# A token store on another queue, token sums in smaller pieces, a square on DVE, and first loads of the second product inside the last pair

## The chip, the cores and the metric

The kernel runs on one core of a Trainium2 chip, in fp32. The metric is the device time of one execution in microseconds, as the median over several runs. The core has five engines with ordered queues: PE (matrix products), DVE (vector operations), ACT (activations, and here also the rounding copies), POOL (further vector operations) and SP, which in this kernel only issues DMA transfers. An instruction waits at the head of its engine's queue, and all that is behind it waits too.

## What is computed

One layer of a diffusion backbone on 1152 tokens (128 of context, 1024 latent), width 1024. The change touches its last third. `mix` is the sum of two gated branches; then, with a layer norm `LN`:

```
x  = LN(ALPHA*x + gate1 * (mix @ w_out)) * ln_g[0] + ln_b[0]      # kept as x2
u  = LN(x) * (1 + scale2) + shift2
hid = square(relu(u @ w_fc + b_fc))                                # 1152 x 4096
x  = LN(ALPHA*x + gate2 * (hid @ w_proj + b_proj)) * ln_g[1] + ln_b[1]
```

## The kernel before

Products in fp32 precision are made of three passes of a rounded type: every operand is split into `hi`, a rounded copy made by ACT (line 67 in `split`, line 1053 for u), and `lo`, the rest, made by a subtraction on DVE or POOL (lines 68, 1055). `mm3` (lines 111 to 113) then issues hi x hi, hi x lo and lo x hi. The order of all instructions is written out by hand; within an engine they run in the order in which the program issues them.

*Output projection* (`branches`, from line 1011). For each of nine token tiles t, `wout(t)` issues 48 matmuls, then `cols(t-3)`, `chain(t)` and `chain2(t-1)`. `chain` loads the old x (`xr`, SP, line 988), multiplies by the gate and adds (DVE, 994 and 995), takes the statistics, normalises (ACT) and applies ln_g and ln_b (POOL, 999 and 1000; DVE for the last tile). `chain2` stores x2 (SP, 1005), takes new statistics and normalises into `z`. `cols` turns z by eight transposes on PE (1044), scales and shifts into `u` (ACT 1051, from tile 6 on half of it on DVE 1049), makes hi (ACT 1053), stores u to DRAM in `u_d` (SP, 1054) and returns the lo part (DVE 1055), which `wout` issues after `chain`. z has three buffers, u one. The tiles 6 to 8 are turned later, between the first groups of the first feed-forward product, which are issued at the end of `branches` (1069 to 1079).

*First feed-forward product* (`ffn1`). The 32 column blocks of w_fc go in 16 pairs. The first two pairs are plain products: six groups remain here, each ended by a relu and a square on ACT (1149, 1150); a pair is stored to `h_d` on SP (1095). Pairs 2 to 15 use seven products instead of eight on 2x2 blocks (a Strassen scheme in the Winograd form), which need sums of token blocks (`Th`, `Tl`) and of weight blocks. The token sums are the generator `sums(s)`, s the half of the tokens: four loads of quarters of u_d (1111), four differences of 128x1152 elements (1118) and their hi and lo parts (1122 on ACT, 1124 on POOL or DVE). Four steps of the generator are issued behind each of the six groups, the rest behind the store of pair 1. Then come the first weights of pair 2 (`load`, 1167; `prep`). For a pair, `steps` lists 14 products, each with what follows it: copies of a bank (`keep`, ACT 1239), adds (DVE 1248), relus (ACT 1092), and `end`, the square of one half of the tokens (ACT 1253, 128x1152). Each is followed by `store`.

*Second feed-forward product* (`ffn2`). It runs in eight blocks b of four k tiles. `ahead(b)` loads four rows of h into the buffer of the lo parts (1291), then, four times, a weight (1300, two staging buffers `ws`) and its split, and the split of one row of h. `ahead(0)` is issued whole ahead of the first product, behind the bias `bp` (1281).

```
for _ in ahead(0):
    pass
```

Of the kernel before, what the change touches and what calls it, by code (L numbers as in the profile page):

```python
# [9 lines left out]
F = mybir.dt.float32  # L10
R = mybir.dt.float32r
# [28 lines left out]
class Kern:  # L40
# [871 lines left out]
    def branches(self, st, hrp):  # L912
# [90 lines left out]
        def chain2(t):  # L1003
            y = ys.pop(t)
            nc.sync.dma_start(self.x2_d[t], y)
            mv = self.ln_stats(y)
            z = p3.tile([128, D], F, name="z", tag="z", bufs=3)
            self.normalise(z, y, mv)
            xn[t] = z

# [20 lines left out]
        def cols(t, bank=self.pj):  # L1031
            c, o = t // 3, (t % 3) * 128
            if t % 3 == 0:
                h, l = self.hilo(c)
                self.hi.append(h)
                self.lo.append(l)
            z = xn.pop(t)
            u = p3.tile([128, KT, 128], F, name="u", tag="u", bufs=1)
            j = 1 if t else 0
            for g in range(2):  # L1040
                tp = bank()
                for i in range(4):
                    k = 4 * g + i
                    nc.tensor.transpose(tp[:, i * 128:(i + 1) * 128], z[:, k * 128:(k + 1) * 128], self.ident)
                for i in range(4):
                    k = 4 * g + i
                    q = tp[:, i * 128:(i + 1) * 128]
                    if t >= 6 and g == 1:
                        nc.vector.tensor_scalar(u[:, k, :], q, m2[:, 1, k, j:j + 1], m2[:, 0, k, j:j + 1], OP.mult, OP.add)
                    else:  # L1050
                        nc.scalar.activation(u[:, k, :], q, AF.Identity, scale=m2[:, 1, k, j:j + 1], bias=m2[:, 0, k, j:j + 1])  # L1051
            h, l = self.hi[c][:, :, o:o + 128], self.lo[c][:, :, o:o + 128]
            nc.scalar.activation(h, u, AF.Copy)
            nc.sync.dma_start(self.u_d[:, :, t * 128:(t + 1) * 128], u)
            return lambda: nc.vector.tensor_tensor(l, u, h.bitcast(F), OP.subtract)  # L1055

        self.hi, self.lo = [], []
# [24 lines left out]
    def ffn1(self, st):  # L1082
# [18 lines left out]
        self.r0s.close()  # L1101
        pt = self.pool(st, "tt")
        Th, Tl = [pt.tile([128, 4, 4, 2 * HN], R, name=n) for n in ("Th", "Tl")]
        tmp = ExitStack()
        ptmp = self.pool(tmp, "tmp")
        B = lambda a, k, s, j: a[:, 4 * k:4 * k + 4, 2 * HN * s + HN * j:2 * HN * s + HN * j + HN]

        def sums(s):
            f = lambda a, i: a.bitcast(F)[:, i, :, HN * s:HN * s + HN]
            for o, k, j in ((f(Tl, 0), 0, 1), (f(Th, 0), 0, 0), (f(Tl, 1), 1, 1), (f(Th, 3), 1, 0)):  # L1110
                nc.sync.dma_start(o, B(self.u_d, k, s, j))
            yield
            g, v = nc.gpsimd, nc.vector
            d = {}

            def diff(i, x, y, e):
                d[i] = ptmp.tile([128, 4, HN], F, name="T", tag="T", bufs=3)
                e.tensor_tensor(d[i], x, y, OP.subtract)

            def part(i, e):  # L1120
                h, l = Th[:, i, :, HN * s:HN * s + HN], Tl[:, i, :, HN * s:HN * s + HN]
                nc.scalar.activation(h, d[i], AF.Copy)
                yield
                e.tensor_tensor(l, d[i], h.bitcast(F), OP.subtract)
                yield

            diff(2, f(Tl, 1), f(Tl, 0), g)
            yield
            diff(0, f(Tl, 0), f(Th, 0), v)
            yield  # L1130
            diff(1, f(Tl, 1), d[0], v)
            yield
            yield from part(2, g)
            yield from part(0, v)
            diff(3, f(Th, 3), d[1], v)
            yield
            yield from part(1, g)
            yield from part(3, v)

        work = (x for s in range(2) for x in sums(s))  # L1140
        for p in range(2):
            for i in range(2):
                w = self.fcw[2 * p + i] if 2 * p + i < 3 else self.w_next(("fc", 3), 0)
                for c in range(NC):
                    if c < 2 and 2 * p + i < 3:
                        continue
                    ps = self.group(w, c)
                    o = Hs[p][:, i, c * C:(c + 1) * C]
                    relu(o, ps, 2 * p + i)
                    nc.scalar.activation(o, o, AF.Square)  # L1150
                    for _ in range(4):
                        next(work, None)
            store(p, Hs[p])
        for _ in work:
            pass
        tmp.close()
        pe = self.pool(st, "ev")


        raw, ready, pos = {}, [], [None, 0]  # L1160
# [49 lines left out]
        def need(n):  # L1210
            while len(ready) < n and next(weights, 0) is None:
# [5 lines left out]
        P = {1: ("A11", pair(0, 0)), 5: ("S1", tt(0)), 6: ("S2", tt(1)), 7: ("S3", tt(2)),  # L1217
             2: ("A12", pair(1, 0)), 4: ("A22", tt(3)), 3: ("S4", pair(1, 1))}
        need(8)
        for p in range(2, 16):  # L1220
            H = new_h()
            base = 7 * (p - 2)
# [27 lines left out]

            def end(s):
                q = H[:, :, 2 * HN * s:2 * HN * s + 2 * HN]
                nc.scalar.activation(q, q, AF.Square)

            steps = [(1, 0, "A", True, lambda: keep(1, 0)), (1, 1, "A", True, lambda: keep(1, 1)),
                     (5, 0, "C", True, None), (6, 0, "A", False, lambda: keep(2, 0)),
# [9 lines left out]
            for i, (n, s, b, first, after) in enumerate(steps):  # L1266
                mul(n, s, b, first)
                if after:
                    after()
                if i % 2:  # L1270
                    need(base + 8 + i // 2 + 1)
            store(p, H)


    def ffn2(self, st):
        nc, I, O = self.nc, self.I, self.O
        self.lo_pool = False
        p = self.pool(st, "ffn")
        acc = [p.tile([128, D], F, name=f"acc{t}") for t in range(NT)]
        bp = p.tile([128, D], F, name="bp", tag="bp")  # L1280
        nc.sync.dma_start(bp, I["b_pr"].to_broadcast([128, D]))
        rows = {}
        gate = lambda t: rows["g2l" if t else "g2c"]
        x2s = {}
        ws = {}
        NS = 8

        def load_h(b):
            for i in range(4):
                o = 4 * (b % 2) + i  # L1290
                nc.sync.dma_start(self.X[1][:, o, :].bitcast(F), self.h_d[2 * b + i // 2][:, i % 2, :])

        def split_h(b, i):
            o = 4 * (b % 2) + i
            h, l = self.X[0][:, o, :], self.X[1][:, o, :]
            self.split(h, l, l.bitcast(F))

        def weight(b, i):
            s = self.ring.tile([128, 1024], F, name="ws", tag="ws", bufs=2)
            nc.sync.dma_start(s, I["w_pr"][4 * b + i])  # L1300
            if b % 2:
                w = p.tile([128, 2, 1024], R, name="w", tag="w2", bufs=4)
            else:
                w = self.ring.tile([128, 2, 1024], R, name="w", tag="w", bufs=4)
            self.split(w[:, 0], w[:, 1], s, nc.gpsimd if b else None)
            ws[b, i] = w

        def ahead(b):
            if b >= NS:
                return  # L1310
            load_h(b)
            yield
            for i in range(4):
                weight(b, i)
                yield
                split_h(b, i)
                yield

        def proj(b, t):
# [21 lines left out]
            if t:  # L1341
                nc.vector.scalar_tensor_tensor(acc[t - 1], x2s.pop(t - 1), ALPHA, acc[t - 1], OP.mult, OP.add)

        for _ in ahead(0):
            pass
        sa = ExitStack()
        self.sides.append(self.ada_rest(self.pool(sa, "ada"), range(6, 8)))
        for b in range(NS - 1):
# [130 lines left out]
```

## Time and profile before

| | us |
|---|---|
| median of 3 runs | 2325.74 (2325.53 to 2326.64) |
| the profiled execution | 2322.08 |
| its span, first to last instruction | 2320.0 |
| PE busy | 2161.7 (93%) |
| DVE, ACT, POOL busy | 1289.8, 947.2, 650.9 (56%, 41%, 28%) |
| mean granted clock of PE | 0.972 |

Times of the trace count from the start of the span. In the rows, `PE pj L112` is a matmul of line 112 into the tile `pj`; `SPq` is SP's queue of transfers; `[12.06 <-DVE lo L1055]` means that the engine was idle for 12.06 us before, and that an instruction of line 1055 on DVE ended it. The clock is a share of full speed (1.00 is the 2.4 GHz level, 0.50 the 1.2 GHz one). A matmul's length in the timeline is longer than its distance to the next one, since they overlap.

### The profile page before, as it was taken

The page shows a single profiled execution, that of the slowest core. Times are in us where ns is not written, and L with a number is a line of the kernel's source. Part 1 is how long each engine was busy: PE and PEld are TensorE (multiplying, and loading weights), DVE is VectorE, ACT ScalarE, POOL GpSimd, SP SyncE. Part 2 cuts the span into 40 slices and gives each one's busy share as a digit, 9 for nine tenths or more (in the row PEclk, how much of TensorE's full clock was granted, in tenths as well). Part 3 has the DMA queues.
Part 4 walks back from the last instruction along what each step waited for, and adds up shares of the span by engine and source line. Part 5 has one row for each costly group of instructions (what it writes and reads, how often), then busy time and mean ns, then how long its engine had stood idle before and what let it go on. Part 6 is the DMA issues. An engine that isn't in the chain of part 4 may idle for free.

```text
span 2320.0 us, 31633 instructions
## 1 busy us (share of the span) xinstructions
PE 2161.7 (93%) x12723; PEld 2031.2 (88%) x12723; DVE 1289.8 (56%) x2096; ACT 947.2 (41%) x1500; POOL 650.9 (28%) x349
## 2 busy tenths in 40 slices
PE   7988999999999999999899998589999969999996
PEld 4888999999999999999899987579999958888885
DVE  4364775775674546887625465552333326643378
ACT  5454424414524426777613234354555441121112
POOL 1402212311420312233302042343333302331176
PEclk9999999999999999999999999789999979999998
DMA  6121241142122130111432323352222244322342
GB/s 265 37 70 38 71 142 54 61 135 75 60 94 79 41 96 28 46 46 67 154 97 88 141 83 102 98 177 87 95 100 101 93 153 146 114 95 78 128 145 82
DMA packets 96754, 223.83 MB, mean 96 GB/s; under 512 B 20132, under 2 KB 48420, under 8 KB 93536
## 3 DMA queue, kind: packets, MB, share of 16 engines
q1 hardware_dynamic: 84368, 209.16, 26.8%
q10 hardware_dynamic: 12240, 12.66, 1.6%
q8 instruction: 99, 1.62, 0.3%
q14 instruction: 47, 0.39, 0.1%
HBM read 171.70 MB, written 50.09 MB: 96 GB/s over the span
## 4 chain that ended last, share of the span: by engine, by line
PE 74%; DVE 8%; DMA 6%; ACT 3%; issue 2%; SPq 1%; POOL 0%; ACTq 0%; DVEq 0%
PE pj L111 16%; PE pj L112 16%; PE pj L113 16%; PE pps L113 5%; PE pps L112 5%; PE pps L111 5%; DMA out_n<-nt 2%; PE xb L111 1%; PE xb L112 1%; PE xb L113 1%; DMA xr<-in_x 1%; PE wps L113 1%; PE wps L112 1%; PE wps L111 1%; ACT u L1051 1%
## 5 line engine op out<-in xcount | busy, mean ns | idle before, releaser
L111 PE MATMUL pj<-hi,w 128*128 128x384 f32 (+1 forms) x2120 | 706.4, 333 | 23.6 <-ACT w L67 9.4
L112 PE MATMUL pj<-lo,w 128*128 128x384 f32 (+1 forms) x2120 | 703.2, 332 | 20.4 <-DVE lo L1055 12.1
L113 PE MATMUL pj<-hi,w 128*128 128x384 f32 (+1 forms) x2120 | 702.4, 331 | 0.8 <-POOL w L68 0.8
L111 PEld LDWEIGHTS pj<-hi,w 128*128 128x128 f32 x2120 | 404.3, 191 | 26.1 <-ACT u L1051 10.0
L112 PEld LDWEIGHTS pj<-lo,w 128*128 128x128 f32 x2120 | 404.2, 191 | 21.2 <-DVE lo L1055 12.3
L113 PEld LDWEIGHTS pj<-hi,w 128*128 128x128 f32 x2120 | 403.9, 190 | 1.2 <-POOL w L68 1.2
L68 POOL TENSOR_TENSOR w<-ws,w 128x1024 fp32r<-128x1024 f32 (+1 forms) x91 | 184.1, 2028 | 573.8 <-ACT w L67 531.7
L67 ACT ACTIVATE w<-ws 128x1024 fp32r<-128x1024 f32 (+1 forms) x175 | 159.0, 914 | 379.8 <-DMA ws<-in_w_pr 282.5
L111 PE MATMUL pps<-w,hi 128*128 128x512 f32 x576 | 225.5, 391 | 19.9 <-ACT hi L67 19.9
L113 PE MATMUL pps<-w,lo 128*128 128x512 f32 x576 | 225.4, 391 | 1.4 <-DVE lo L68 1.4
L112 PE MATMUL pps<-w,hi 128*128 128x512 f32 x576 | 225.2, 391 | 0.0
L68 DVE TENSOR_TENSOR w<-ws,w 128x1024 fp32r<-128x1024 f32 (+1 forms) x84 | 104.8, 1254 | 113.6 <-ACT w L67 112.7
L1334 DVE TENSOR_TENSOR acc<-pps,acc 128x512 f32<-128x512 f32 x108 | 73.7, 690 | 142.9 <-PE pps L113 142.9
L111 PEld LDWEIGHTS pps<-w,hi 128*128 128x128 f32 x576 | 108.8, 189 | 42.9 <-ACT hi L67 20.5
L111 PE MATMUL pj<-Th,w 128*128 128x288 f32 x448 | 134.2, 300 | 9.3 <-ACT e L1239 9.3
L112 PE MATMUL pj<-Tl,w 128*128 128x288 f32 x448 | 132.7, 296 | 0.0
L113 PE MATMUL pj<-Th,w 128*128 128x288 f32 x448 | 132.6, 296 | 0.0
L113 PEld LDWEIGHTS pps<-w,lo 128*128 128x128 f32 x576 | 108.6, 189 | 25.5 <-DVE lo L68 3.2
L112 PEld LDWEIGHTS pps<-w,hi 128*128 128x128 f32 x576 | 108.8, 189 | 22.7
L716 POOL TENSOR_TENSOR CS<-Cst,CS 128x516 fp32r<-128x516 f32 x56 | 74.2, 1326 | 184.1 <-ACT CS L715 180.2
L1248 DVE TENSOR_TENSOR Hf<-pj,e 128x288 f32<-128x288 f32 x84 | 36.6, 454 | 143.5 <-ACT e L1239 88.7
L464 POOL PARTITION_ALL_REDUCE aacc<-aacc x16 | 56.2, 3556 | 195.4 <-DVE aacc L463 169.4
(313 smaller groups left out, 4082.5 us busy)
## 6 DMA issues: line engine op xcount, KB each, us to landing
ws<-in_w_in SPq DMA_DIRECT2D x56, 512.0 KB, 4.1
h<-Hf SPq DMA_DIRECT2D x16, 1152.0 KB, 4.8
lo<-h SPq DMA_DIRECT2D x32, 576.0 KB, 3.8
aw<-in_w_ada SPq DMA_DIRECT2D x64, 256.0 KB, 3.6
ws<-in_w_fc SPq DMA_DIRECT2D x32, 512.0 KB, 3.4
ws<-in_w_pr SPq DMA_DIRECT2D x32, 512.0 KB, 4.2
gm<-gs ACTq DMA_DIRECT2D x48, 192.0 KB, 1.9
gmr<-gm SPq DMA_DIRECT2D x16, 576.0 KB
```

The source lines that it names most:

```text
L67: self.nc.scalar.activation(hi, x, AF.Copy)
L68: (eng or self.nc.vector).tensor_tensor(lo, x, hi.bitcast(F), OP.subtract)
L111: mm(out, lhsT=ah, rhs=bh, start=first, stop=False, skip_group_check=onto)
L112: mm(out, lhsT=ah, rhs=bl, start=False, stop=False, skip_group_check=onto)
L113: mm(out, lhsT=al, rhs=bh, start=False, stop=last, skip_group_check=onto)
L464: nc.gpsimd.partition_all_reduce(acc[j], acc[j], channels=128, reduce_op=ReduceOp.add)
L716: nc.gpsimd.tensor_tensor(CS[d][1], Cst[d], CS[d][0].bitcast(F), OP.subtract)
L1051: nc.scalar.activation(u[:, k, :], q, AF.Identity, scale=m2[:, 1, k, j:j + 1], bias=m2[:, 0, k, j:j + 1])
L1248: nc.vector.tensor_tensor(o, bank[b, s][:, :HN], ev[e, s], OP.add)
L1334: nc.vector.tensor_tensor(acc[t][:, s], pss[n], (acc[t] if b else bp)[:, s], OP.add)
```

## The change

Four edits. The store of u is issued by ACT's queue, and u is written into the buffer of z, which now has four buffers (before: three of z and one of u). The token sums are made per k tile, in pieces of 128x288, with tiles of the pool `ev`, and five steps of the generator are issued behind each group. The square at the end of a half pair is a product on DVE. The helpers of the second product become methods, and in the last pair (p = 15) `early(i)` issues, behind step i, the four loads of h (i = 1), the splits of its four rows (6, 8, 10, 12) and the first two weights with their splits (7, 10); the other two weights are issued at the start of `ffn2`, behind the load of `bp`.

```diff
     def chain2(t):
-            z = p3.tile([128, D], F, name="z", tag="z", bufs=3)
+            z = p3.tile([128, D], F, name="z", tag="z", bufs=4)
     def cols(t, bank=self.pj):
             z = xn.pop(t)
-            u = p3.tile([128, KT, 128], F, name="u", tag="u", bufs=1)
+            u = z.rearrange("p (k t) -> p k t", t=128)
...
             nc.scalar.activation(h, u, AF.Copy)
-            nc.sync.dma_start(self.u_d[:, :, t * 128:(t + 1) * 128], u)
+            nc.scalar.dma_start(self.u_d[:, :, t * 128:(t + 1) * 128], u)
...
-        tmp = ExitStack()
-        ptmp = self.pool(tmp, "tmp")
+        pe = self.pool(st, "ev")
     def sums(s):
...
-            d = {}
-
-            def diff(i, x, y, e):
-                d[i] = ptmp.tile([128, 4, HN], F, name="T", tag="T", bufs=3)
-                e.tensor_tensor(d[i], x, y, OP.subtract)
-
-            def part(i, e):
-                h, l = Th[:, i, :, HN * s:HN * s + HN], Tl[:, i, :, HN * s:HN * s + HN]
-                nc.scalar.activation(h, d[i], AF.Copy)
-                yield
-                e.tensor_tensor(l, d[i], h.bitcast(F), OP.subtract)
-                yield
-
-            diff(2, f(Tl, 1), f(Tl, 0), g)
-            yield
-            diff(0, f(Tl, 0), f(Th, 0), v)
-            yield
-            diff(1, f(Tl, 1), d[0], v)
-            yield
-            yield from part(2, g)
-            yield from part(0, v)
-            diff(3, f(Th, 3), d[1], v)
-            yield
-            yield from part(1, g)
-            yield from part(3, v)
+            for k in range(4):
+                q = lambda a, i: f(a, i)[:, k, :]
+                d = {}
+
+                def diff(i, x, y, e):
+                    d[i] = pe.tile([128, HN], F, name="e", tag="e", bufs=6)
+                    e.tensor_tensor(d[i], x, y, OP.subtract)
+
+                def part(i, e):
+                    h, l = (a[:, i, k, HN * s:HN * s + HN] for a in (Th, Tl))
+                    nc.scalar.activation(h, d[i], AF.Copy)
+                    e.tensor_tensor(l, d[i], h.bitcast(F), OP.subtract)
+
+                diff(2, q(Tl, 1), q(Tl, 0), g)
+                diff(0, q(Tl, 0), q(Th, 0), v)
+                diff(1, q(Tl, 1), d[0], v)
+                yield
+                diff(3, q(Th, 3), d[1], v)
+                part(2, g)
+                part(0, v)
+                yield
+                part(1, g)
+                part(3, v)
+                yield
...
                     nc.scalar.activation(o, o, AF.Square)
-                    for _ in range(4):
+                    for _ in range(5):
                         next(work, None)
             store(p, Hs[p])
         for _ in work:
             pass
-        tmp.close()
-        pe = self.pool(st, "ev")
...
+        def early(i):
+            if i == 1:
+                self.load_h(0)
+            if i in (6, 8, 10, 12):
+                self.split_h(0, (i - 6) // 2)
+            if i in (7, 10):
+                self.weight(0, (i - 7) // 3)
...
             def end(s):
                 q = H[:, :, 2 * HN * s:2 * HN * s + 2 * HN]
-                nc.scalar.activation(q, q, AF.Square)
+                nc.vector.tensor_tensor(q, q, q, OP.mult)
...
                 if i % 2:
                     need(base + 8 + i // 2 + 1)
+                if p == 15:
+                    early(i)
             store(p, H)
...
+    def load_h(self, b):
+        for i in range(4):
+            o = 4 * (b % 2) + i
+            self.nc.sync.dma_start(self.X[1][:, o, :].bitcast(F), self.h_d[2 * b + i // 2][:, i % 2, :])
+    def split_h(self, b, i):
+        o = 4 * (b % 2) + i
+        h, l = self.X[0][:, o, :], self.X[1][:, o, :]
+        self.split(h, l, l.bitcast(F))
+    def weight(self, b, i):
+        s = self.ring.tile([128, 1024], F, name="ws", tag="ws", bufs=2)
+        self.nc.sync.dma_start(s, self.I["w_pr"][4 * b + i])
...
+        self.split(w[:, 0], w[:, 1], s, self.nc.gpsimd if b else None)
+        self.ws2[b, i] = w
     def ffn2(self, st):
...
-        for _ in ahead(0):
-            pass
+        self.weight(0, 2)
+        self.weight(0, 3)
```

## Rows read from the trace of the kernel before

**Rows 1.** Busy time by stretch: from:to, length, PE, PEld, DVE, ACT, POOL, PEclk, DMA, GB/s

```profile
1426.00:1512.00 86.00, 54.48 (x233) 47.37 (x234) 46.52 (x73) 38.17 (x69) 25.90 (x9) 0.80 0.32 98
1567.00:1885.00 318.00, 310.85 (x2316) 308.57 (x2316) 95.03 (x148) 159.65 (x311) 103.98 (x78) 1.00 0.24 90
1885.00:1915.00 30.00, 8.74 (x23) 5.56 (x23) 10.25 (x9) 10.04 (x10) 0.00 (x0) 0.60 0.75 270
```

**Rows 2.** Timeline of PE: start, length, line, matmul; in brackets the idle before

```profile
1500.72 0.69 PE L112 MATMUL pj<-lo,w 128*128 128x384 f32 x1 [12.06 <-DVE lo L1055]
...
1555.75 0.61 PE L111 MATMUL pj<-hi,w 128*128 128x288 f32 x1 [9.45 <-ACT w L67]
...
1904.91 0.80 PE L111 MATMUL pps<-w,hi 128*128 128x512 f32 x1 [19.89 <-ACT hi L67]
```

**Rows 3.** Chain of waits in the output projection: start, length, what

```profile
1390.65 0.87 PE pj L1044 x8
1402.44 0.88 PE pj L1044 x8
...
1431.70 5.12 DMA xr<-in_x
1436.91 1.24 DVE y L995
...
1445.46 2.91 ACT u L1051 x8
1448.96 5.30 DMA xr<-in_x
...
1490.08 1.24 DVE y L995
```

**Rows 4.** Waits of SP's queue, 1390 to 1520: total, times, longest

```profile
SPq L1054 <- ACT u L1051: 76.9, 7, 15.3
```

**Rows 5.** Timeline of SP's queue in the output projection

```profile
1414.24 15.63 SPq L62 DMA_DIRECT2D ws<-in_w_fc  x2
...
1448.39 0.52 SPq L1054 DMA_DIRECT2D u_d<-u  x1
...
1449.72 1.02 SPq L1005 DMA_DIRECT2D x<-y  x1
```

**Rows 6.** Timeline of POOL: a product-stage sum and one of the sums

```profile
1444.22 3.29 POOL L1000 TENSOR_TENSOR y<-y,bn 128x1024 f32<-128x1024 f32 x1
...
1536.80 3.30 POOL L1124 TENSOR_TENSOR Tl<-T,Th 128x1152 fp32r<-128x1152 f32 x1 [0.45 <-ACT Th L1122]
```

**Rows 7.** Timeline of DVE: two differences of the sums

```profile
1527.04 1.36 DVE L1118 TENSOR_TENSOR T<-Tl,Th 128x1152 f32<-128x1152 f32 x1 [6.76 <-DMA Th<-u_d]
...
1537.49 3.83 DVE L1118 TENSOR_TENSOR T<-Th,T 128x1152 f32<-128x1152 f32 x1
```

**Rows 8.** Groups by form: count, busy us, mean ns, idle before

```profile
L1248 DVE TENSOR_TENSOR Hf<-pj,e 128x288 f32<-128x288 f32 x84 | 36.6, 454 | 143.5 <-ACT e L1239 88.7 <-PE pj L113 54.8
...
L68 POOL TENSOR_TENSOR w<-ws,w 128x512 fp32r<-128x512 f32 x42 | 56.4, 1343 | 136.1 <-ACT w L67 136.1
```

**Rows 9.** Timeline of ACT at both passages

```profile
1547.45 0.56 ACT L1092 ACTIVATE Hf<-pj,pack 128x384 f32<-128x384 f32 x1
...
1555.07 0.63 ACT L67 ACTIVATE w<-ws 128x512 fp32r<-128x512 f32 x1 [1.29 <-DMA ws<-in_w_fc]
...
1902.74 1.06 ACT L67 ACTIVATE w<-ws 128x1024 fp32r<-128x1024 f32 x1 [15.47 <-DMA ws<-in_w_pr]
```

**Rows 10.** Timeline of SP's queue at both passages

```profile
1549.02 1.34 SPq L1167 DMA_DIRECT2D ws<-in_w_fc  x2
...
1866.52 21.10 SPq L1095 DMA_DIRECT2D h<-Hf  x2
1887.66 0.44 SPq L1281 DMA_DIRECT2D bp<-in_b_pr  x1
...
1892.33 1.17 SPq L1300 DMA_DIRECT2D ws<-in_w_pr  x2
```

More of the change, by code (lines that the diff above doesn't have):

```diff
@@ L1219, in ffn1 @@
         need(8)
+        self.ws2 = {}
+        def early(i):
[5 more added lines that the diff above has]
+                self.weight(0, (i - 7) // 3)
         for p in range(2, 16):
@@ L1271, in ffn1 @@
                     need(base + 8 + i // 2 + 1)
+                if p == 15:
+                    early(i)
             store(p, H)
+    def load_h(self, b):
[9 more added lines that the diff above has]
+        self.nc.sync.dma_start(s, self.I["w_pr"][4 * b + i])
+        if b % 2:
+            w = self.p2.tile([128, 2, 1024], R, name="w", tag="w2", bufs=4)
+        else:
+            w = self.ring.tile([128, 2, 1024], R, name="w", tag="w", bufs=4)
+        self.split(w[:, 0], w[:, 1], s, self.nc.gpsimd if b else None)
+        self.ws2[b, i] = w
     def ffn2(self, st):
@@ L1277, in ffn2 @@
         self.lo_pool = False
-        p = self.pool(st, "ffn")
+        p = self.p2 = self.pool(st, "ffn")
         acc = [p.tile([128, D], F, name=f"acc{t}") for t in range(NT)]
@@ L1284, in ffn2 @@
         x2s = {}
-        ws = {}
+        ws = self.ws2
         NS = 8
[L1288 to L1306, printed above, removed]
         def ahead(b):
-            if b >= NS:
-                return
-            load_h(b)
+            self.load_h(b)
             yield
             for i in range(4):
-                weight(b, i)
+                self.weight(b, i)
                 yield
-                split_h(b, i)
+                self.split_h(b, i)
                 yield
```

## Prediction

> **What bounds the kernel now.** I first read the busy line of the page: PE works for 93% of the span, so only the places where it stands still can be won. The stretch table names them: the stage of the output projection (PE busy 54.48 of 86 us, clock 0.80) and the passage between the two feed-forward products (8.74 of 30 us, clock 0.60) [rows 1]. The PE timeline then gives the large holes and what ended them: 12.06 us before the lo part of the sixth token tile, 9.45 us before the first weight of the pairs, 19.89 us before the second product [rows 2].
>
> The chain of waits says why the first stage is slow. Its period is one load of x: 1431.70 to 1448.96 is 17.26 us, of which xr takes 5.12; then y, its statistics, z, then u on ACT (1445.46 + 2.91 = 1448.37), and at 1448.96 the next xr starts [rows 3]. SP shows the link: the store of u goes out at 1448.39, and only behind it comes the load [rows 5]; that store waited on ACT's u seven times, 76.9 us in all [rows 4]. So a load which needs nothing of u is released by u. Without this, one tile costs PE 11.79 us (1390.65 to 1402.44, while PE was ahead) [rows 3].
>
> **The change part by part.**
>
> *Token store on ACT's queue, u written into z.* SP's order becomes xr(t), x2(t-1), xr(t+1). x2(t-1) needs POOL's sum, some 10.6 us behind y's start (1436.91 to 1444.22 + 3.29) [rows 3, 6]; but this loop spans two tiles, so with 1 us of issue and 5.3 us of load it asks for about 8.5 us per tile. The engines' own orders: on DVE the way from y (1436.91) to where ACT takes u up (1445.46) is 8.55 us [rows 3], with the gate multiplies (as many columns as y, so some 1.3) about 9.9; ACT has u 2.91, hi (1024 columns, as the split of 1.06 [rows 9]), the issue of the store 0.53 (SP's price [rows 5]) and under 6 for y, z and two roots, 10.3 us. Both lie under PE's 11.79. So PE sets the pace: the product of tile 3 ends at 1390.65, that of tile 8 at 1390.65 + 5 x 11.79 = 1449.6. One hitch remains: SP's two weight loads at 1414.24 hold the queue 15.63 us, because the second waits for a DVE split [rows 5]; tile 5's xr stays behind it. I put that split at about 1416 in the new order, so y of tile 5 comes near 1422.5 instead of 1415; with a DVE order of 9.9 us against 11.79 three tiles win back most of it, and y of tile 8 comes at 1452.5 against 1490.08 [rows 3]: 37.6 us earlier. What follows (the lo part that ends the 12.06 us hole) keeps its order. That hole shrinks to 2 to 4 us and gives back some 1.4 us of half clock. Store waits of u in the three late tiles (about 2 us each) hid under PE and bring nothing. Sum: -39 us; -34 if DVE and POOL collide once per tile, -43 if PE never stands still.
>
> *Sums in pieces.* Before, DVE and POOL had 16 operations of 1152 columns; now they have 64 of 288. DVE and POOL keep each other out: DVE's subtraction costs 1.36 alone and 3.83 from 1537.49; POOL's began at 1536.80 and ended at 1540.10, and 1540.10 + 1.36 is close to DVE's end at 1541.32 [rows 6, 7]. So their times add. Each k piece has five DVE operations of 0.454 and three of POOL; POOL's nearest row is 1.34 for 512 columns, 0.78 if it scales to 288 [rows 8]. 5 x 0.454 + 3 x 0.78 = 4.6, with handoffs 4.85, for eight pieces 38.8 us. They begin where DVE's first sum did, 1527.04 [rows 7], plus some 1.4 because the load into Tl should now wait for the landing of the last u (it overlays z): end near 1567.
> That alone PE would not feel, as it needs the sums only six steps into the pair. But five pieces per group instead of four are now issued, 25 of 26 of them ahead of the last group's relu on ACT's ordered queue. Before, that relu ran at 1547.45 [rows 9]; now it stands behind the hi parts of the last k piece, about 1564. Behind it come the square, the store of the pair, and on SP the first weight load of the pairs (1549.02), whose landing (1555.07) ended PE's hole [rows 9, 10]. All move by 16.5 us; collisions with the sums saved later give back 1 to 1.5. Sum: +15. Bounds: +4 if DVE and POOL overlapped fully, +27 if a small POOL operation cost the whole 1.34.
>
> *Square on DVE.* 28 squares of 1152 columns, 1.36 each [rows 7], 38 us on DVE, which is busy 95.03 of 318 in the pairs, while PE is busy 310.85 [rows 1]. PE's short stalls there wait on ACT's copies behind weight splits, not on squares. Cost 0; if DVE's cover were gone, at most the 0.2 us by which it is longer than ACT's at the last store, and a wait for POOL of up to 1.3; taken together -2 to +2.
>
> *First loads and splits in the last pair.* The cost before: the square ends, the pair's store goes out, bp at 1887.66, four loads of h, and the weight load at 1892.33; its split starts at 1902.74 [rows 9, 10]. Now the four h loads leave right behind the store of the pair before (1866.52 [rows 10]; the first two steps of the pair have read the buffer). The old train of bp, four loads and a weight behind a store took 1887.66 to 1902.74, 15.1 us; without bp I take 13.5, so the first weight lands near 1880. From there ACT's and DVE's queues are one ping-pong, because each split stands ahead of the pair's own adds and relus: w 1.06 and hi 1.2 by its columns on ACT [rows 9], lo 1.36, w 1.24 as y's [rows 3], adds 0.454, two squares 1.36 on DVE [rows 7, 8]: 11 us of DVE, 17 with the handoffs. The step that reuses the bank of the last copy is met to within 1 us. But the last store leaves at 1897 instead of just ahead of 1887.66, and the third weight stands behind it and bp on SP: half of the old train, 7.5 us, so 1904.5, split by 1905.6. PE does the first half of the first product early (2.7 us), waits, and ends its 24 matmuls near 1911 against 1915.6. Sum: -4.5. Bounds: -12 if the handoffs cost nothing and the store is not late; +2 if the first weight lands 3 us later and PE waits for the copy in the pair.
>
> **Total.** -39 + 15 + 0 - 4.5 = -28.5 on the profiled execution's 2322.08: 2293.6. The median of the runs lies 3.66 above that execution, so the prediction is 2297 for it.
>
> **Rivals.**
> *Only the issue time is saved (slower).* If xr merely found another thing ahead of it, x2 of the tile before, the period would stay: xr 5.9, y to POOL's end 10.6, issue 1, 17.5 us. Then moving nine stores saves 9 x 0.53 = 4.8 us and the rest gives -4.8 + 15 - 4.5 = +5.7: 2331. It decides as soon as the stage wins less than 10.5 us. For it: x2 is on the same queue. Against: it goes out at 1449.72, right behind xr [rows 5], and the next xr is a tile later. The Trainium skill (DMA: Bandwidth & Descriptors, Issuing engines are not separate DMA queues) says that starting transfers from several engines saves only the sequencer's time to start them, usually small; by that rule this rival would hold. The row of the 76.9 us wait speaks against it, since here the queue's order, not its issue time, is the cost.
> *The sums stay cheap.* DVE and POOL interleave at this size and T costs +4: 2286. For it: the pieces let ACT start sooner; against: the 3.83 us row.
> *The passage closes.* The splits hide wholly and PE waits only for the last two weights: -15 there, 2287. Against: the third weight is still behind the last store.
> *u in place binds PE to ACT.* If the second four transposes waited for the first four u's, as both touch one buffer, the loop would be 11.1 of products, 1.5 of u and about 1.1 of transposes, 13.7 us: five tiles lose up to 9.5, less the 2.9 that tile 5 lost anyway: 2304.
>
> **Chances.** My forecast 0.5, with its own range 2285 to 2311; cheap sums 0.18; closed passage 0.12; in-place wait 0.1; issue time only 0.06; others 0.04. Range: 2277 to 2314, which takes in the first four and leaves the tails of the POOL price and of the slower rival. 0.2% (4.7 us) is about what a measurement of this kernel tells from no change. Faster 0.90, same 0.04, slower 0.06.
>
> **What would show it.** Right: xr loads leave without u ahead, about 11.8 us apart, and the hole before the lo part is under 4 us; the last relu of the groups runs some 16 us behind PE's last group and the hole of 9.45 grows to about 25; the second product starts its first four blocks directly behind the last pair and then waits 14 us for the third weight. Wrong: xr still 17 us apart; the hole before the pairs at 9 to 14 us; the last store at its old distance from the last matmul.

## The result and the profile after

The changed kernel takes 2290.2 us (median of 4 runs, 2287.31 to 2291.59), the kernel before 2326.19 beside it (4 runs): a ratio of 0.9844, 95% interval 0.9827 to 0.9861, so 36 us faster. The prediction was 2297 with a range of 2277 to 2314. The profiled execution of the changed kernel took 2287.31 us, its span is 2285.5 against 2320.0.

The three stretches of [rows 1], of the same lengths and, to within about 1 us, at the same places of the work, which now come earlier by 37, 29 and 31 us:

```profile
1389.00:1475.00 86.00, 81.89 (x407) 71.59 (x406) 66.50 (x102) 52.83 (x98) 36.37 (x13) 0.96 0.42 135
1538.00:1856.00 318.00, 310.00 (x2322) 307.79 (x2322) 138.37 (x177) 135.35 (x287) 115.30 (x78) 1.00 0.27 100
1854.00:1884.00 30.00, 13.02 (x36) 9.04 (x35) 11.38 (x12) 8.74 (x11) 0.44 (x1) 0.60 0.56 205
```

In the output projection PE is now busy 81.89 of 86 us at a clock of 0.96, against 54.48 at 0.80. In the pairs, DVE went from 95 to 138 us busy and ACT from 160 to 135: the squares and, at the end, the splits. In the passage to the second product PE still stands for more than half of the 30 us.

The timeline of PE has the holes that answer to [rows 2]:

```profile
1463.78 0.69 PE L112 MATMUL pj<-lo,w 128*128 128x384 f32 x1 [4.11 <-DVE lo L1055]
...
1527.00 0.61 PE L111 MATMUL pj<-hi,w 128*128 128x288 f32 x1 [17.58 <-ACT w L67]
...
1856.87 0.50 PE L111 MATMUL pps<-w,hi 128*128 128x512 f32 x1 [1.74 <-ACT w L67]
...
1874.64 0.80 PE L111 MATMUL pps<-w,hi 128*128 128x512 f32 x1 [13.70 <-ACT w L67]
```

12.06 became 4.11; 9.45 became 17.58; and the one wait of 19.89 became three, 1.74, 1.08 and 13.70, of which the last stands in the middle of the first product.

SP's queue in the output projection, beside [rows 5]:

```profile
1403.12 12.83 SPq L62 DMA_DIRECT2D ws<-in_w_fc  x2
1416.01 0.42 SPq L988 DMA_DIRECT2D xr<-in_x  x1
1416.52 0.38 SPq L1005 DMA_DIRECT2D x<-y  x1
1417.00 0.38 SPq L988 DMA_DIRECT2D xr<-in_x  x1
...
1432.68 0.37 SPq L988 DMA_DIRECT2D xr<-in_x  x1
...
1443.19 0.38 SPq L988 DMA_DIRECT2D xr<-in_x  x1
```

No store of u stands between the loads of x any more. The one thing that still holds them is the pair of weight loads, 12.83 us. With it DVE waits for a load of x once, 3.61 us, and three tiles later it has caught up: y of tile 8, whose row was 1490.08 in [rows 3], comes at 1452.58.

```profile
1421.54 1.23 DVE L995 SCALAR_TENSOR_TENSOR y<-xr,y 128x1024 f32<-128x1024 f32 x1 [3.61 <-DMA xr<-in_x]
...
1452.58 1.78 DVE L995 SCALAR_TENSOR_TENSOR y<-xr,y 128x1024 f32<-128x1024 f32 x1
```

ACT's queue at the start of the pairs, beside [rows 9]: the relu of the last group now stands behind hi parts of the sums (line 1123), several of which wait for a difference.

```profile
1515.44 1.01 ACT L1123 ACTIVATE Th<-e 128x288 fp32r<-128x288 f32 x2 [0.54 <-DVE e L1119]
1517.98 0.78 ACT L1123 ACTIVATE Th<-e 128x288 fp32r<-128x288 f32 x2 [1.54 <-POOL e L1119]
1518.67 0.56 ACT L1092 ACTIVATE Hf<-pj,pack 128x384 f32<-128x384 f32 x1
1519.26 0.52 ACT L1148 ACTIVATE Hf<-Hf 128x384 f32<-128x384 f32 x1
1519.69 0.76 ACT L1123 ACTIVATE Th<-e 128x288 fp32r<-128x288 f32 x2
1526.32 0.63 ACT L67 ACTIVATE w<-ws 128x512 fp32r<-128x512 f32 x1 [5.87 <-DMA ws<-in_w_fc]
```

PE's last group had ended at 1509.43, so the relu is 9.2 us late (before: 1.15). Behind the square, on SP, go the store and the load of the first weight, beside [rows 10]; and at the end of the pairs the store of the last pair, bp, and the third and fourth weight:

```profile
1519.81 0.33 SPq L1095 DMA_DIRECT2D h<-Hf  x1
1520.25 1.34 SPq L1163 DMA_DIRECT2D ws<-in_w_fc  x2
...
1864.53 0.33 SPq L1095 DMA_DIRECT2D h<-Hf  x1
1864.94 0.38 SPq L1310 DMA_DIRECT2D bp<-in_b_pr  x1
1865.42 2.11 SPq L1296 DMA_DIRECT2D ws<-in_w_pr  x2
```

### The profile page after: what moved, and what is told of

Same layout as the page of the kernel before. It is cut to its first block, busy times and chain, and to the rows that moved or that the text cites. A ratio compares the mean times of both kernels' runs of the same rounds, so it can differ in the third digit from the quotient of the medians.

```text
span 2285.5 us, 31722 instructions
## 1 busy us (share of the span) xinstructions
PE 2150.3 (94%) x12723; PEld 2021.9 (88%) x12723; DVE 1333.9 (58%) x2154; ACT 922.3 (40%) x1496; POOL 666.7 (29%) x367
## 5 line engine op out<-in xcount | busy, mean ns | idle before, releaser
L112 PEld LDWEIGHTS pj<-lo,w 128*128 128x128 f32 x2120 | 402.7, 190 | 12.5 <-DVE lo L68 8.1
L1341 DVE TENSOR_TENSOR acc<-pps,acc 128x512 f32<-128x512 f32 x108 | 73.7, 691 | 146.6 <-PE pps L113 146.5
L111 PEld LDWEIGHTS pj<-Th,w 128*128 128x128 f32 x448 | 84.0, 188 | 11.5 <-ACT e L1246 11.5
```

The costliest lines, as they stand in the source:

```text
L111: mm(out, lhsT=ah, rhs=bh, start=first, stop=False, skip_group_check=onto)
L112: mm(out, lhsT=ah, rhs=bl, start=False, stop=False, skip_group_check=onto)
L1341: nc.vector.tensor_tensor(acc[t][:, s], pss[n], (acc[t] if b else bp)[:, s], OP.add)
```

## Experiments

Each experiment is the changed kernel with the edit shown. The runs were made on three chips. On these the kernel before took 2328 us instead of 2326, and in the experiments' traces the first load of x came at 1358 to 1365 us instead of 1354, with nothing edited ahead of it. So the ratios are compared with that of the changed kernel run again on the last chip (0.9851), and the traces by stages that begin at that load. All lengths are us, from PE's and SP's timelines: A from the first load of x to the sixth lo part (the 4.11 us hole's end), B to the first matmul of the pairs, C to the first matmul that uses the third weight of the second product (to the first of all where nothing was early), D to the end of the span.

| kernel | A | B | C | D | A to D | ratio (95%) |
|---|---|---|---|---|---|---|
| before | 146.6 | 55.0 | 349.2 | 415.1 | 965.8 | 1 |
| changed | 109.7 | 63.2 | 347.6 | 410.9 | 931.4 | 0.9844 (0.9827 to 0.9861) |
| changed, again | 110.1 | 63.4 | 349.5 | 409.8 | 932.8 | 0.9851 (0.9838 to 0.9865) |
| store on SP | 147.0 | 63.3 | 347.9 | 410.6 | 968.7 | 1.0017 (1.0008 to 1.0026) |
| u its own buffer | 109.8 | 66.3 | 347.7 | 410.7 | 934.5 | 0.9875 (0.9859 to 0.989) |
| sums whole | 109.9 | 54.4 | 349.6 | 410.5 | 924.4 | 0.9828 (0.981 to 0.9846) |
| square on ACT | 109.5 | 63.4 | 350.7 | 410.7 | 934.3 | 0.9878 (0.9857 to 0.9898) |
| no early loads | 110.2 | 63.5 | 348.4 | 415.1 | 937.2 | 0.987 (0.9855 to 0.9884) |
| four steps | 110.1 | 57.3 | 349.6 | 410.5 | 927.5 | 0.9828 (0.9812 to 0.9845) |
| load ahead of store | 110.6 | 57.5 | 349.5 | 410.8 | 928.3 | 0.9841 (0.9826 to 0.9855) |
| weights ahead | 109.2 | 63.4 | 337.0 | 411.0 | 920.6 | 0.9807 (0.9793 to 0.9822) |
| sums on DVE | 110.4 | 59.5 | 349.5 | 409.5 | 928.9 | 0.9834 (0.9821 to 0.9848) |
| three edits | 110.8 | 57.6 | 337.1 | 410.0 | 915.5 | 0.9785 (0.9771 to 0.9798) |
| splits first | 110.1 | 53.9 | 344.7 | 410.1 | 918.9 | 0.9793 (0.9779 to 0.9806) |

A, B and D repeat within 1.6 us where an edit does not touch them. In C two profiles of the changed kernel itself differ by 1.9, so a difference of that size is put to no edit. The ratios hold the part ahead of the first load too, which varies more: on the chip of the kernels with four steps and with the load ahead of the store alone, that load came at 1358.37 in the one trace and at 1365.06 in the other. So a gain that the stages show need not be found whole in the ratio.

**The control.**

> The changed kernel itself, for comparison on this chip. If the parts ahead of the output projection differ from chip to chip (the first load of x came at 1354.1 us in the two traces of the first chip, at 1358 to 1365 in the experiments), its ratio here is 0.985 to 0.987 instead of 0.9844, and its stages from the first load of x on have the same lengths within 1 us.

0.9851, as expected; A and B agree within 0.4 us, D within 1.1 and C within 1.9, somewhat more than expected. Of the 5.9 us by which this trace is longer than the first one, 4.5 lie ahead of the first load of x.

**The store back on SP.**

```
-            nc.scalar.dma_start(self.u_d[:, :, t * 128:(t + 1) * 128], u)
+            nc.sync.dma_start(self.u_d[:, :, t * 128:(t + 1) * 128], u)
```

> The changed kernel with the nine token stores of u put back on SP; u still lies in z. Theory (the order of SP's queue was the cost): the load of x of the next tile again leaves only behind the store of u, the x loads of the late tiles are about 17 us apart, the store's issue waits on ACT's u for some 70 to 77 us in all, the hole before the sixth lo part is 11 to 12 us again instead of 4.1, and the time is 34 to 38 us above the changed kernel's 2290, so 2324 to 2328. Rival (u in z won it, since the next u no longer waits for a landing): the x loads stay 11 to 12 us apart and the time stays within 5 us of 2290. Second rival (only the nine issues of 0.53 us count): 2295.

Stage A is 147.0 again, 37.3 more than in the changed kernel, and the ratio is 1.0017: with this one word undone the rest of the change gains nothing. The waits of SP's queue (total, times, longest) have the row of [rows 4] again, and SP's timeline the old order and the old 17.4 us between two loads:

```profile
SPq L1054 <- ACT z L1051: 77.8, 7, 15.8
```

```profile
1455.40 0.66 SPq L988 DMA_DIRECT2D xr<-in_x  x1
...
1472.18 0.53 SPq L1054 DMA_DIRECT2D u_d<-z  x1
1472.81 0.60 SPq L988 DMA_DIRECT2D xr<-in_x  x1
```

The order of SP's queue is the cause; both rivals are out. The measured median, 2332.4, is above the expected 2324 to 2328, which was put beside the first 2290; it is 38.5 above the control's 2293.9, where 34 to 38 was expected.

**u in a buffer of its own, the store on ACT.**

```
-            z = p3.tile([128, D], F, name="z", tag="z", bufs=4)
+            z = p3.tile([128, D], F, name="z", tag="z", bufs=3)
-            u = z.rearrange("p (k t) -> p k t", t=128)
+            u = p3.tile([128, KT, 128], F, name="u", tag="u", bufs=1)
```

> The changed kernel with u in a buffer of its own (one, as before) and three buffers of z; the store stays on ACT's queue. Theory (queue order): the gain stays, 2288 to 2293, the hole before the sixth lo part 4 to 5 us; the next tile's u waits for the landing of the store for at most 1 us, as the tiles are 11.8 us apart. Rival (u in z was half of it): the next u waits for the store's landing by several us a tile, the x loads are 14 us or more apart and the time is 2300 to 2315.

Stage A is unchanged (109.8), so the queue alone did that. But the median, 2298.62, is above the expected range, and B is 3 us longer, which no theory had: in the last two tiles, which follow each other closely, ACT waits for the landing of the store before it may overwrite u (8.1 us, the longest 6.0), and PE for ACT. The waits of ACT's queue between 1400 and 1500, and PE's timeline:

```profile
ACT u L1051 <- DMA u_d<-u: 8.1, 2, 6.0
```

```profile
1493.07 0.45 PE L111 MATMUL pj<-hi,w 128*128 128x384 f32 x1 [2.27 <-ACT hi L1053]
```

**The sums as before.**

```
-                    d[i] = pe.tile([128, HN], F, name="e", tag="e", bufs=6)
+                d[i] = ptmp.tile([128, 4, HN], F, name="T", tag="T", bufs=3)
...
-                    for _ in range(5):
+                    for _ in range(4):
```

> The changed kernel with the token-side sums as before: whole operations of 1152 columns, buffers of their own, four steps a group. Theory (the pieces put the last groups' relu behind the last hi parts on ACT): the last relu of the groups comes 1 to 2 us behind PE's last group instead of 9.2, the hole before the pairs is 9 to 10 us instead of 17.57, and the time is 6 to 9 us lower, 2281 to 2284. Rival (the sums themselves are late either way, since their loads now come sooner after the last store of u): the hole stays at 14 us or more and the time within 3 us of 2290.

PE's hole is 9.37 us and B 9.0 shorter than in the control. The ratio falls by 0.0023, 5 us, less than the expected 6 to 9, and its interval overlaps the control's; it is the trace that carries the reading. The edit as a whole, pieces and five steps a group, was a loss in this kernel. Beside the next experiment, where the pieces stay and the fifth step goes (B 57.3), 6.1 us of it come from the fifth step and 2.9 from the pieces.

**Four steps a group, pieces kept; and the load ahead of the store.** Two ways to break the chain of relu, square, store and load at different links.

```
-                    for _ in range(5):
+                    for _ in range(4):
```

> The changed kernel with four steps of the sums issued after each group instead of five; the pieces stay. Theory (the last relu stands on ACT behind the hi parts of the last pieces): the last relu runs 1 to 3 us behind PE's last group instead of 9.2, the store of the pair leaves some 7 us sooner, and the hole before the pairs is 10.5 to 12.5 us instead of 17.57, not less, because the split of the first weight now stands behind the last hi parts on ACT: 5 to 7 us of gain, ratio 0.9815 to 0.9825. Rival (the sums' own time sets the hole, in whatever order): the hole stays over 16 us and the ratio at 0.984.

```
+            if p:
+                load(2)
             store(p, Hs[p])
...
-        load(2)
         weights = prep()
```

> The changed kernel with the first weight load of the pairs issued on SP ahead of the store of the second pair; five steps a group as changed. Theory (relu, square, store and load stand in one chain, and the hole ends with the load's landing, 6 us behind its issue): the load lands while the sums still run, and the hole is set by ACT's queue alone: the split of the first weight runs right behind the last square, at about 1520.5 on the changed kernel's scale, and the hole is 11.5 to 12.5 us instead of 17.57; ratio 0.9815 to 0.9825. Rival (the store's transfer and the load share the same engines, so that the load's landing is no earlier): the hole stays above 16 us.

The holes are 12.25 and 12.39 us, B 6.1 and 5.9 shorter than in the control. In the first the relu runs at 1517.41, 3.9 us behind PE's last group (1 to 3 were expected), with eight hi parts behind it instead of two; but the split of the first weight still stands behind the last of these. ACT's timeline:

```profile
1517.41 0.56 ACT L1092 ACTIVATE Hf<-pj,pack 128x384 f32<-128x384 f32 x1
...
1524.72 0.44 ACT L1123 ACTIVATE Th<-e 128x288 fp32r<-128x288 f32 x1 [0.52 <-DVE e L1119]
1525.10 0.63 ACT L67 ACTIVATE w<-ws 128x512 fp32r<-128x512 f32 x1
```

In the second the load left at 1510.24, 21.7 us ahead of the store (SP's timeline), and the split still runs only at 1532.49, directly behind the last two hi parts, with no wait for a load in its row (ACT's):

```profile
1510.24 2.07 SPq L1145 DMA_DIRECT2D ws<-in_w_fc  x2
1531.94 0.33 SPq L1095 DMA_DIRECT2D h<-Hf  x1
```

```profile
1531.82 0.76 ACT L1123 ACTIVATE Th<-e 128x288 fp32r<-128x288 f32 x2
1532.49 0.61 ACT L67 ACTIVATE w<-ws 128x512 fp32r<-128x512 f32 x1
```

So the hole has two possible ends, about 6 us apart: the landing of a load behind the store, and ACT's ordered queue. Removing the first uncovers the second. Of the 6 us that each trace shows, the ratios keep 5 (0.9828) and 2 (0.9841), the latter with an interval that holds both; 0.9815 to 0.9825 was expected of each.

**All sums on DVE.**

```
-            g, v = nc.gpsimd, nc.vector
+            g, v = nc.vector, nc.vector
```

> The changed kernel with all sums of the token side on DVE, none on POOL. The page of the changed kernel has 3.83 us a k piece with five operations on DVE and three on POOL. Theory (DVE's and POOL's operations keep each other out, so their times add, less a fixed part that overlaps): eight operations on DVE at 0.45 take 3.6 us a piece; the sums end within 2 us of their time in the changed kernel, the hole before the pairs is 15 to 18 us, and the time stays within 2.5 us. Rival (POOL's share runs beside DVE's and the rows of DVE are long for another reason, such as waits inside them): DVE's operations stay at 0.7 to 0.9 us, a piece takes 5.6 us or more and the hole grows to 25 us or more.

The hole is 14.53 against 18.32 in the control beside it, and the ratio 0.9834 against 0.9851, with intervals that overlap. DVE alone does the eight operations of a k piece in 3.20 us (1499.20 to 1502.40); with three of them on POOL it took 3.85 (two pieces from 1494.15 to 1501.86). Groups of DVE's operations by form, 1488 to 1535 (count, busy us, mean ns, idle before), first of the changed kernel, then of this one:

```profile
L1124 DVE TENSOR_TENSOR Tl<-e,Th 128x288 fp32r<-128x288 f32 x16 | 13.1, 839 | 0.8 <-ACT Th L1123 0.3
L1119 DVE TENSOR_TENSOR e<-Tl,Th 128x288 f32<-128x288 f32 x7 | 5.5, 791 | 0.0
```

```profile
L1124 DVE TENSOR_TENSOR Tl<-e,Th 128x288 fp32r<-128x288 f32 x32 | 12.5, 452 | 0.1
L1119 DVE TENSOR_TENSOR e<-Tl,Th 128x288 f32<-128x288 f32 x8 | 3.6, 453 | 0.0
```

The same subtraction takes 839 ns beside POOL and 452 without. So the rival is out. The theory holds, but I had expected less of it (a hole of 15 to 18 us, a time within 2.5 us; the median is 3.7 lower): POOL's help costs DVE more (3.85 less five operations at 0.40, an eighth of 3.20, is 1.85 us a piece) than doing POOL's three operations itself (1.2).

**The square on ACT.**

```
-                nc.vector.tensor_tensor(q, q, q, OP.mult)
+                nc.scalar.activation(q, q, AF.Square)
```

> The changed kernel with the squares of the pairs back on ACT. Theory (hidden on either engine): the time stays within 2 us of 2290; the pairs take 326 to 328 us. Rival (the square on ACT delayed the copies that PE waits for; its move was worth the 2.5 us by which the stage of the pairs became shorter): the stage takes 329 us or more and the time is 2292 to 2294. In the last pair the squares and the splits then share ACT: if the early splits are held up by it, the hole before the second half of the first product grows from 13.7 to 15 us or more.

The median is 2297.83, which is more than either had; but the ratio is 0.9878 against 0.9851, with intervals that overlap, and of the trace only a part can be put to the square. PE's timeline has, once in two pairs, a short wait for an ACT copy; from one to the next is 45.87 us with the square on ACT and 45.76 with it on DVE (first this kernel, then the changed one), 0.11 in two pairs and 0.8 in all fourteen.

```profile
1603.06 0.40 PE L111 MATMUL pj<-Th,w 128*128 128x288 f32 x1 [1.02 <-ACT e L1246]
1648.93 0.41 PE L111 MATMUL pj<-Th,w 128*128 128x288 f32 x1 [1.02 <-ACT e L1246]
```

```profile
1594.47 0.40 PE L111 MATMUL pj<-Th,w 128*128 128x288 f32 x1 [1.02 <-ACT e L1246]
1640.23 0.40 PE L111 MATMUL pj<-Th,w 128*128 128x288 f32 x1 [1.02 <-ACT e L1246]
```

The stage of the pairs is 329.06 us against 327.85 in the control and 326.74 in the changed kernel's first trace, which is what the rival asked for (329 or more). But some 1.5 us of it are a stretch at half clock in the first pair (granted clock 0.66 from 1545 to 1550, 1.00 in the control's 1543 to 1548), and the traces of five kernels with the square on DVE have this stretch too, with stages of 328.4 to 328.6 us: sums whole, no early loads, four steps, load ahead of store, sums on DVE. So the trace puts 0.8 us to the square, and the rival is not borne out. The hole in the second product is 14.96 against 14.04 in the control. Why the ratio is higher by as much as 0.0027 (6 us) stays open; of the 3.8 us between the two traces, 2.3 lie ahead of the first load of x.

**No early loads.**

```
-                if p == 15:
-                    early(i)
...
-        self.weight(0, 2)
-        self.weight(0, 3)
+        for _ in ahead(0):
+            pass
```

> The changed kernel without the early loads and splits: all loads of h and all four weights of the second product are issued after the last pair, as before. Theory (their move saved the difference of the passage, some 3 us, because the third weight still stands behind the last store): PE waits once, 18 to 20 us, before the second product, its stretch from the last pair to the end is 2.5 to 4.5 us longer than in the changed kernel, and the ratio to the kernel before is 0.9855 to 0.9865 against 0.9844. Rival (the splits in the last pair held PE up as much as they saved): the same ratio within 0.0007.

PE waits once, 19.87 us, as before. C and D together are 763.4 against 759.4 in the control and 758.5 in the changed kernel's first trace: 4.1 to 4.9 longer, and 0.0019 by the ratios (4.4 us), whose intervals overlap. The ratio itself came out above the expected one because that was put beside 0.9844.

**The third and fourth weight ahead of the last store.**

```
+            if i in (12, 13):
+                self.w_load(0, i - 10)
+            if i == 13:
+                self.w_split(0, 2)
+                self.w_split(0, 3)
...
-        self.weight(0, 2)
-        self.weight(0, 3)
```

Here w_load and w_split are the two halves of weight.

> The changed kernel with the loads of the third and fourth weight of the second product issued ahead of the last pair's store (in its steps 12 and 13) and their splits in its last step. Theory (the 13.7 us hole is the third weight's load, which stands on SP behind the last store and bp): the hole shrinks to 3 to 5 us, the time falls by 8 to 11 us, ratio 0.980 to 0.981. Rival (the hole is set by the splits on ACT and DVE, which are busy with the last pair's sums, relus and squares): the hole stays above 9 us and the gain below 5 us.

The hole shrinks from 14.04 in the control to 4.25, C by 10.6 to 12.5 us, and the ratio falls by 0.0044, 10 us. PE's timeline has the hole; SP's, behind it, has all four loads leaving between 1844 and 1863 and the store 6 us later. So the place on SP behind the late store was the cost; the rival is out.

```profile
1868.62 0.80 PE L111 MATMUL pps<-w,hi 128*128 128x512 f32 x1 [4.25 <-ACT w L67]
```

```profile
1844.08 19.18 SPq L1305 DMA_DIRECT2D ws<-in_w_pr  x4
1869.04 0.33 SPq L1095 DMA_DIRECT2D h<-Hf  x1
```

**Four steps, load ahead and weights ahead together.**

> The changed kernel with three of the edits together: four steps a group, the first weight load of the pairs ahead of the store of the second pair, and the third and fourth weight of the second product ahead of the last store. Theory: the hole before the pairs falls no lower than the two edits alone brought it (12.24 and 12.39 us), as both leave the split of the first weight behind the last hi parts on ACT: 11 to 12.5 us; the hole in the second product is 4 to 5 us. Together 14 to 17 us below the changed kernel on the same chip. Rival (the two front edits add up, each removing its own 5 us): the hole before the pairs is 6 to 8 us and the gain 19 to 22 us.

The median is 2279.0, ratio 0.9785: 15 us below the control on the same chip, 49 below the kernel before, and the lowest of all. The two front edits do not add up: the hole before the pairs is 12.63 us, as with either alone (the expected bound was 12.5). The second hole is 3.16.

```profile
1527.23 0.61 PE L111 MATMUL pj<-hi,w 128*128 128x288 f32 x1 [12.63 <-ACT w L67]
...
1864.33 0.80 PE L111 MATMUL pps<-w,hi 128*128 128x512 f32 x1 [3.16 <-ACT w L67]
```

**And the first splits ahead of the rest of the sums.**

```
+        need(3)
         for _ in work:
             pass
```

The functions that load and split the pairs' weights are moved in front of these lines.

> As the kernel with the three edits together, and besides the first three splits of the pairs' weights are issued ahead of the rest of the sums instead of behind them. Theory (ACT's order is all that is left of the hole): the split of the first weight runs right behind the last square, 2 to 4 us behind PE's last group, and the hole is 3 to 5 us; the second half's sums now come later by the two weight sums and the splits on DVE and POOL, so PE waits again in the first pair, where the fifth step needs them: 5 to 9 us there. Net 1 to 5 us below the kernel with the three edits. Rival (what PE saves at the hole it loses whole in the first pair, since the sums set the pace): within 2 us of it.

Ratio 0.9793: no gain over the three edits, as the rival had it, though not for its reason. The hole is only down to 8.88 (3 to 5 was expected), because four steps of the sums are already issued behind the last relu. And what is won at B (3.7 us) is lost in C (7.6), in the first pair, where PE waits 6.15 us; not for the sums, but for a copy on ACT that stands behind the split of the next pair's first weight, which itself waits for its load. PE's timeline, then ACT's:

```profile
1526.34 0.61 PE L111 MATMUL pj<-hi,w 128*128 128x288 f32 x1 [8.88 <-ACT w L67]
...
1542.29 0.61 PE L111 MATMUL pj<-Th,w 128*128 128x288 f32 x1 [6.15 <-ACT e L1253]
```

```profile
1541.31 0.63 ACT L67 ACTIVATE w<-ws 128x512 fp32r<-128x512 f32 x1 [4.56 <-DMA ws<-in_w_fc]
1541.85 0.69 ACT L1253 ACTIVATE e<-pj 128x288 f32<-128x288 f32 x2
```

A kernel with the three edits and the sums on DVE alone was not run; the two act on the same hole, so their gains need not add up.

## Why the prediction was right, step by step

- *Token store (predicted -39).* Right in mechanism and size. From the first load of x to the sixth lo part the trace is 36.8 us shorter (146.56 to 109.72; counted from the start of the span, the lo part comes 36.9 earlier). y of the sixth tile came at 1421.54 (predicted near 1422.5), y of tile 8 at 1452.58 (predicted 1452.5). The hole itself, 4.11 us, lies just above the predicted 2 to 4. The 1.4 us of half clock that it was to give back, for which the prediction showed no row, did not come: the 23 matmuls behind it took 6.43 us, behind the larger hole 6.36. By the Trainium skill's rule (DMA: Bandwidth & Descriptors, Issuing engines are not separate DMA queues), which was the slower rival, only the time to start the transfers is saved; nine stores at 0.52 us are 4.7. The trace does not agree, as 37.3 us hang on the one word of the first experiment: the rule counts the issue, not what waits in order behind the issue.
- *Sums in pieces (predicted +15).* This is the mis-sized term: hole from 9.45 to 17.58, +8.1, and 9.0 by the experiment that undoes it. Its steps, in order: the start of the sums was right (the first difference ran at 1487.46, but the next waited for its load until 1490.31, and the train runs from there; predicted was 1527.04 + 1.4 - 37.6 = 1490.8); the relu behind the last pieces was right; the price of a piece was not, 3.85 us instead of 4.85, eight times. So the relu came 9.2 us behind PE instead of 16. I had added POOL's three operations at 0.78 (scaled from 1.34 for 512 columns, which would be 0.75) to DVE's five at 0.454 and put handoffs on top; measured, a POOL operation of 288 columns took 0.8 to 1.1, but cost DVE only 0.6 (1.85 for three). The Trainium skill (SBUF — State Buffer, Who interferes with whom) says that a DVE instruction with two inputs in SBUF contends with a GpSimd one that reads SBUF; the 839 and 452 ns agree.
- *Rival "the sums stay cheap".* Its time was nearer the mark (2286) than my sum, but its reason is not what happened: DVE and POOL did not interleave for nothing, and DVE had almost no idle time between 1492 and 1521.
- *Square on DVE (predicted 0, -2 to +2).* 0.8 us by the period of the pairs. The rest of the 2.5 us by which the stage of the pairs became shorter in the two traces (329.27 to 326.74) is mostly half clock behind a hole: the 48 matmuls behind the second small hole took 8.05 us before (granted clock 0.68 in the first 5 us) and 6.62 after (1.00). That is not the square's doing, since five of the experiments' traces with the square on DVE have the stretch as well; the prediction had no term for it, and what brings it stays open. The second trace of the changed kernel has none either; its stage is 1.1 us longer mainly by a wait of PE of 0.66 us for an ACT copy late in the last pair.
- *First loads and splits in the last pair (predicted -4.5).* -4.1 to -4.9 by undoing it. As written, PE did the first half of the product early and then waited 13.70 us (predicted 14) for the third weight behind the last store; the two short waits in that half, 1.74 and 1.08 us for splits, were not predicted.
- *Rival "u in place binds PE to ACT".* It did not: PE kept 11.78 us a tile (transposes at 1390.36, 1402.14, 1413.91, 1425.68). By the traces, in place was even worth 3 us at the end.
- *Total.* -36.9 + 8.1 - 2.5 - 3.2 = -34.5, which is the difference of the spans (2320.0 to 2285.5; the last term as the two traces show it). The predicted -28.5 was 6.0 short: the sums give 6.9 of this, the stage of the pairs 2.5 (0.8 the square, the rest mostly the half clock, which was luck), the store -2.1 and the early loads -1.3.

## What to carry to other kernels

In an ordered queue, ask of every transfer what stands ahead of it and not what it needs: the load of x needed nothing of u and lost 37 us behind its store, and the same question found 10 us more at the second product. When steps are spread between groups, see what the last group's own work then stands behind on each engine, and expect that breaking one link of the chain uncovers the next, here after about 6 us. Before you share small two-input operations between DVE and POOL, time them on DVE alone.

## What I had not expected of the hardware

- Three of eight 288-column subtractions moved to POOL made the piece longer, 3.85 us against 3.20 on DVE alone.
- Removing a hole does not always shorten the half clock behind it (6.43 us against 6.36 for the same 23 matmuls behind 4.11 and 12.06 us), and two traces of one kernel differ by 1.9 us from the start of the pairs to the third weight of the second product. Behind the small hole in the first pair some traces have a stretch at half clock, which costs some 1.5 us (holes of 2.18 to 3.60 us), and others none (2.25 to 2.91).
- The unedited part ahead of the first load of x took 4 to 11 us more in the experiments' traces (1358.4 to 1365.1 against 1354.1). These two ends come from one chip, so the chip alone does not explain it. The stages A, B and D agreed within 1.6 us where nothing was edited.
